# Input projection weights split by a casting DMA and an accumulating DMA

## The chip, the cores and the metric

The kernel runs on one core of one Trainium2 chip. The metric is the device time of one launch in microseconds (us). PE is TensorE's matmul, PEld its weight load, DVE is VectorE, ACT is ScalarE, POOL is GpSimd, SP is SyncE, which here only issues DMAs.

## What is computed

One decoder block over 1024 tokens of width 1024: a LayerNorm, one combined input projection to 5648 columns, a state-space branch and a convolution branch on its columns, one output projection, and two norms with a gated per-layer input. What the change touches is the projection:

```
h    = layer_norm(x, ln_emb_g, ln_emb_b)
proj = einsum('bld,de->ble', h, w_in[i])
xs, z, bm, cm, dt_raw, glu, cgate = split(proj, SPLITS)
xbc  = silu(causal_depthwise_conv(concatenate([xs, bm, cm])))      # width 4
u    = (glu[:D] + b) * sigmoid(glu[D:] + b)
u    = silu(layer_norm(causal_depthwise_conv(u, ...)))             # width 31
```

## The kernel before, in words

Everything is float32. A matmul operand is split into two parts: `h` is the operand rounded to the 12 bits that TensorE's fast float32 form (`F32R`) takes, `l` is the exact rest. `three` (L122) then makes one product out of three matmuls: rest by rounded, rounded by rest, rounded by rounded (L123, L124, L125). `split` (L117) makes the two parts: ACT casts (L119), another engine subtracts (L120).

*Input projection.* The weights are 44 tiles of 128 output columns; each is [128, 8, 128] numbers, 512 KB, contiguous per partition in DRAM. `weights(ct)` (L182) takes three slots from a ring of eight (pool `regB`, tag `B2`): `wraw`, `wh`, `wl`. SP loads `wraw`, ACT casts it to `wh`, POOL subtracts to get `wl`. `inproj` (L188) runs 48 matmuls per tile, for two halves of 512 tokens and eight blocks of the input, into a PSUM bank (three banks with that tag), and ACT empties the bank after each half (L262, L265, L296, L373, L383). The input `h` and its parts `hH`, `hL` stay in SBUF.

*What runs beside it.* `ple_all` (L213) projects the per-layer input first; its two `ppraw` tiles take two of the eight slots for a while. `embed` (L159) normalises x (DVE, some on ACT; POOL takes the reciprocal root, L132 and L134), PE transposes it, DVE splits it. Then eight `conf_tile(j)` (L254): two projections each, a gate, and the convolution of width 31, on DVE (L291), but for tiles 1 and 5 as 30 ACT products (L285) and 30 POOL additions (L286). Between them stand two further steps each from a list: `dt_path`, `decays`, twelve `xbc_tile` (short convolution on DVE, L377, then SiLU on ACT, L378, and a store from SP, L379) and `z_tile`. POOL adds up the channel sums `cs` (L628, L630); `conf_norm` (L386) starts with PE's mean of them (L390). Then come the chunked scan and the output projections.

*What sets the order.* Each engine works through its own queue in order; a waiting instruction holds up what stands behind it on its engine. The order in each queue and the semaphores come from a planner that simulates the program when it is built; it can place work of a later step ahead of an earlier one. SP's queue holds all DMA issues of the program.

Of the kernel before, what the change touches and what calls it, by code (L numbers as in the profile page):

```python
# [8 lines left out]
F32 = mybir.dt.float32  # L9
F32R = mybir.dt.float32r  # L10
AF = mybir.ActivationFunctionType
# [3 lines left out]
P = 128  # L15
# [10 lines left out]

# columns of the per-channel vectors
VEC = {}
# [18 lines left out]
def tile_block(ctx: ExitStack, tc: tile.TileContext, x, pT, wple, win, wdt, wout, wgate, vec, rows, heads, out):  # L47
# [17 lines left out]

# [1 line left out]
    BUFS = {"gt": 4, "xd": 2, "u": 2, "ha": 3, "y": 2, "xb": 2, "st": 1}  # L67
# [19 lines left out]

# [1 line left out]
    vc = const.tile([P, NVEC], F32, name="vc")  # L89
# [13 lines left out]
    nc.gpsimd.memset(mhalf, -0.5)  # L103
    # [s, l]: 1 where l >= s
    tri = const.tile([P, P], F32, name="tri")
    nc.gpsimd.affine_select(out=tri, in_=ones, pattern=[[1, P]], compare_op=ALU.is_ge, fill=0.0, base=0, channel_multiplier=-1)
    # adds rows h, 16 + h and 32 + h
    fold = const.tile([P, HEADS], F32, name="fold")
# [8 lines left out]
    def split(src, h, l, leng):  # L117
        """h: src rounded to the tensor engine's 12 bits; l: what is left, exactly."""
        nc.scalar.copy(out=h.bitcast(F32R), in_=src)  # L119
        leng.tensor_tensor(out=l.bitcast(F32R), in0=src, in1=h, op=ALU.subtract)  # L120
# [16 lines left out]
    def moments(src, tag):  # L137
        """mean and rstd of the rows of src [P, 1024]."""
        st = wk.tile([P, 2, 6], F32, name="st" + tag, tag="st" + tag)
        for i in range(2):  # L140
            nc.vector.bn_stats(out=st[:, i, :], in_=src[:, i * 512:(i + 1) * 512])
        mv = small("mv" + tag, 2)
        nc.vector.bn_aggr(out=mv, in_=st)
        return mv[:, 0:1], rstd_of(mv[:, 1:2], 1, tag, nc.gpsimd)
# [6 lines left out]

# [1 line left out]
    xts = [regB.tile([P, D], F32, name="xt", tag="B1") for t in range(NT)]  # L153
# [26 lines left out]

# [1 line left out]
    def weights(ct):  # L182
        raw, wh, wl = (regB.tile([P, NK, P], F32, name=n, tag="B2") for n in ("wraw", "wh", "wl"))
        nc.sync.dma_start(out=raw, in_=win[ct])
        split(raw, wh, wl, nc.gpsimd)
        return wh.bitcast(F32R), wl.bitcast(F32R)
# [13 lines left out]
    def residual():  # L200
        ag, abb, bob = (work(n, "ha") for n in ("ag", "abb", "bob"))
        for i, tl in enumerate((ag, abb, bob)):
            nc.sync.dma_start(out=tl, in_=rows[i:i + 1, :].broadcast_to([P, D]))
        nc.gpsimd.tensor_scalar(out=ag, in0=ag, scalar1=ALPHA, scalar2=0.0, op0=ALU.mult, op1=ALU.add)
        nc.gpsimd.tensor_scalar(out=abb, in0=abb, scalar1=ALPHA, scalar2=0.0, op0=ALU.mult, op1=ALU.add)
        nc.gpsimd.tensor_tensor(out=abb, in0=abb, in1=bob, op=ALU.add)
        # alpha * h + b_out, by tokens
        for t in range(NT):
            nc.gpsimd.tensor_tensor(out=xts[t], in0=xts[t], in1=ag, op=ALU.mult)
            nc.gpsimd.tensor_tensor(out=xts[t], in0=xts[t], in1=abb, op=ALU.add)  # L210
            nc.sync.dma_start(out=ha_d[t], in_=xts[t])

    def ple_all():  # L213
        """the projected per-layer input, by tokens."""
        parts = {}
        tags = iter(["u", "u", "xd", "xd", "gt", "gt", "ha", "ha"])
        for src, nm in ((wple, "wp"), (pT, "pp")):
            for k in range(2):
                raw = work(nm + "raw", "xb") if nm == "wp" else regB.tile([P, L], F32, name=nm + "raw", tag="B2")
                parts[nm, k] = (raw, work(nm + "H", next(tags)), work(nm + "L", next(tags)))  # L220
        for half in range(2):
            hs = slice(half * 512, half * 512 + 512)
            for k in range(2):
                for src, nm in ((wple, "wp"), (pT, "pp")):
                    nc.sync.dma_start(out=parts[nm, k][0][:, hs], in_=src[:, k, hs])
                    split(*(a[:, hs] for a in parts[nm, k]), nc.vector)
        embed_load(0)
        nc.sync.dma_start(out=vc, in_=vec)
        nc.vector.tensor_scalar(out=hb, in0=v("bglu", 0, 16), scalar1=0.5, scalar2=None, op0=ALU.mult)
        parts = {i: (a[1].bitcast(F32R), a[2].bitcast(F32R)) for i, a in parts.items()}  # L230
        for t in range(NT):
            tk = slice(t * P, (t + 1) * P)
            pl = work("pl", "xb" if t % 4 > 1 else "y", L)
            for n in range(2):
                nn = slice(n * 512, n * 512 + 512)
                ps = bank("psp")
                for k in range(2):
                    three(ps, parts["pp", k][0][:, tk], parts["pp", k][1][:, tk], parts["wp", k][0][:, nn], parts["wp", k][1][:, nn], k == 0, k == 1)
                if (t + n) % 2:
                    nc.vector.tensor_copy(out=pl[:, nn], in_=ps)  # L240
                else:
                    nc.scalar.copy(out=pl[:, nn], in_=ps)
            nc.sync.dma_start(out=ple_d[t], in_=pl)
# [10 lines left out]
    def conf_tile(j):  # L254
        """GLU and the causal convolution of 128 channels."""
        ga = work("ga", "gt")
# [44 lines left out]
    def dt_path():  # L301
# [7 lines left out]
        nc.sync.dma_start(out=hd, in_=heads.unsqueeze(0).broadcast_to([P, 2, HEADS]))  # L309
        # both parts of the weights side by side  # L310
        nc.scalar.copy(out=wh2[:, :, 0:HEADS].bitcast(F32R), in_=raw)
# [22 lines left out]

        # softplus(v) = max(v, 0) + 2 atanh(e / (2 + e)), e = exp(-|v|)
        nc.vector.tensor_tensor(out=b3(vv), in0=b3(pst[:, 0:P]), in1=bh(hd[:, 0, :]), op=ALU.add)
# [16 lines left out]
    def decays():  # L353
        """dec holds dt * a at first: its sums over the tokens of each chunk, and what follows from them."""
        ar, er = (wk.tile([P, P], F32, name=n, tag="dg") for n in ("ar", "er"))
# [60 lines left out]
    def out_weight(src, get, tag, last, scale=None, leng=nc.gpsimd):  # L416
        """last: a place for the raw one, where those that share the tag leave none."""
        raw = work("wor", last) if last else get("wor", tag)
        nc.sync.dma_start(out=raw, in_=src)
        h, l = get("woh", tag), get("wol", tag)  # L420
        if scale is None:
            split(raw, h, l, leng)
        else:
            nc.scalar.activation(out=h.bitcast(F32R), in_=raw, func=AF.Copy, scale=scale)
            nc.vector.scalar_tensor_tensor(out=l.bitcast(F32R), in0=raw, scalar=scale, in1=h, op0=ALU.mult, op1=ALU.subtract)
        return h.bitcast(F32R), l.bitcast(F32R)

# [1 line left out]
    state = work("state", "st")  # L429
# [8 lines left out]
    def prep(c):  # L438
        """what chunk c needs besides the state: decays times C.B, x * dt, B by tokens."""
        xb = slabs(work("xb", "xb", 12 * P), 12)  # L440
# [8 lines left out]
        for q in range(2):  # L449
            er = ea_d[c * HEADS:(c + 1) * HEADS, :].rearrange("(t q) l -> q t l", q=2)[q]  # L450
            nc.sync.dma_start(out=ea[q * HD:(q + 1) * HD], in_=er.unsqueeze(0).broadcast_to([HD, NK, P]))
        # exp(acs[l] - acs[s]); the part l < s is held at exp(0) here and dropped with C.B
        for h in range(HEADS):
# [30 lines left out]
    def chunk(c, sz, xb, gg, ea, xdt, xdd, btok):  # L484
        y = slabs(work("y", "y"))
        for g in range(2):
            # from the state, scaled by exp(acs[l])
            ys = y[:, g * 4:g * 4 + 4, :]
# [34 lines left out]
    def mean_square(c, y, ea):  # L523
        """rstd of the two groups of channels of the gated output."""
        sq = ea.rearrange("p (g t) l -> p g t l", g=2)
# [21 lines left out]
    def conf_out(c, mH, mL, ha):  # L547
        """conformer half of the output projection"""
        for n in range(2):
# [14 lines left out]
    def affine(o, src, mu, rs, g, b):  # L564
        """(src - mu) * rs * g + b"""
        nc.vector.scalar_tensor_tensor(out=o, in0=src, scalar=mu, in1=g, op0=ALU.subtract, op1=ALU.mult)
        nc.vector.scalar_tensor_tensor(out=o, in0=o, scalar=rs, in1=b, op0=ALU.mult, op1=ALU.add)

    def out_proj(c, yH, yL):
        """the SSM half of the output projection, and the norm"""  # L570
        r = work("r", "ha")
# [21 lines left out]
    def gate(c, r, hTH, hTL):  # L593
        """the per-layer input, gated, and the norm"""
        pl = work("pl3", "st")
# [75 lines left out]

# [1 line left out]
    ready, last = out_proj(0, *ys.pop(0)), None  # L673
# [58 lines left out]
```

## Time and profile before

| | us |
|---|---|
| median of 3 runs | 932.74 (928.87 to 934.99) |
| profiled execution, span | 927.1 |
| PE busy | 877.1 |
| DVE busy | 708.6 |
| POOL busy | 534.4 |
| ACT busy | 364.8 |

The span goes from the first to the last instruction of the profiled execution; its time outside the span is not in the profile. A busy PE is not a PE at its peak, since matmuls overlap: a matmul's duration in the rows (about 390 ns) is longer than the distance between two starts. An idle time in the rows is put down to what ended it, and a wait for several things to what came last.

### The profile page before, as it was taken

How to read it: one execution, taken by the hardware profiler on the slowest of the kernel's cores; microseconds unless marked ns; L12 is line 12 of the kernel's file. 1: busy time of each engine (PE TensorE's matmuls, PEld its weight loads, DVE VectorE, ACT ScalarE, POOL GpSimd, SP SyncE). 2: the span in 40 equal slices, each digit the busy share in tenths (PEclk: the TensorE clock that was granted, in tenths of full speed). 3: DMA queues.
4: the chain of work that ended last, by engine and by line, in shares of the span. 5: the costliest groups of instructions: out<-in, count | busy, mean ns of one | idle time of the engine just before them, and what ended most of it. 6: DMA issues, size and time to landing. Idle time of an engine off the chain costs nothing.

```text
span 927.1 us, 10959 instructions
## 1 busy us (share of the span) xinstructions
PE 877.1 (95%) x4141; PEld 711.0 (77%) x4141; DVE 708.6 (76%) x830; ACT 364.8 (39%) x513; POOL 534.4 (58%) x298
## 2 busy tenths in 40 slices
PE   6989998989999999999899999999999889999996
PEld 5857787868787888788688887777777668888885
DVE  7868997498999989989626523998885786666665
ACT  3532244665423435555446533644343421111001
POOL 2559836999924249999792254676757442222211
PEclk9999999989999999999999999999999999999999
DMA  9703241321213121322322388888887902222111
GB/s 337 264 24 107 77 157 46 96 69 46 78 37 113 52 86 53 123 97 80 114 100 83 103 304 271 300 273 230 283 264 261 353 25 92 91 90 91 69 46 68
DMA packets 67716, 126.42 MB, mean 136 GB/s; under 512 B 4176, under 2 KB 41552, under 8 KB 67664
## 3 DMA queue, kind: packets, MB, share of 16 engines
q1 hardware_dynamic: 67664, 125.73, 40.4%
q8 instruction: 32, 0.52, 0.2%
q14 instruction: 20, 0.16, 0.1%
HBM read 89.93 MB, written 35.78 MB: 136 GB/s over the span
## 4 chain that ended last, share of the span: by engine, by line
PE 47%; DVE 20%; POOL 13%; DMA 11%; issue 6%; ACT 3%; SPq 1%; POOLq 0%; DVEq 0%; ACTq 0%
POOL acc L286 8%; DVE pc L291 7%; PE ps L123 6%; PE ps L124 6%; PE ps L125 6%; DVE cacc L377 4%; PE psg L123 3%; PE psg L125 3%; PE psg L124 3%; DMA wor<-in_wout_dram 3%; PE pss L123 3%; PE pss L125 3%; PE pss L124 3%; DMA xb<-xbc_d 2%; POOL wl L120 2%
## 5 line engine op out<-in xcount | busy, mean ns | idle before, releaser
L123 PE MATMUL ps<-hH,wl 128*128 128x512 f32 x704 | 278.4, 397 | 12.7 <-ACT ga L262 6.2
L124 PE MATMUL ps<-hL,wh 128*128 128x512 f32 x704 | 278.0, 395 | 1.0 <-DVE hL L179 1.0
L125 PE MATMUL ps<-hH,wh 128*128 128x512 f32 x704 | 278.1, 395 | 0.0
L291 DVE SCALAR_TENSOR_TENSOR pc<-u,vc,pc 128x1024 f32<-128x1024 f32 x174 | 223.8, 1286 | 4.5
L123 PEld LDWEIGHTS ps<-hH,wl 128*128 128x128 f32 x704 | 133.9, 191 | 44.7 <-issue 7.7
L286 POOL TENSOR_TENSOR acc<-acc,prod 128x1024 f32<-128x1024 f32 x60 | 160.2, 2671 | 13.3 <-ACT acc L282 9.3
L124 PEld LDWEIGHTS ps<-hL,wh 128*128 128x128 f32 x704 | 134.2, 191 | 29.3 <-DVE hL L179 1.5
L125 PEld LDWEIGHTS ps<-hH,wh 128*128 128x128 f32 x704 | 134.2, 191 | 28.4 <-issue 0.2
L120 POOL TENSOR_TENSOR wl<-wraw,wh 128x1024 fp32r<-128x1024 f32 x44 | 110.6, 2513 | 53.2 <-ACT wh L119 23.0
L132 POOL TENSOR_SCALAR ve<-mv 128x1 f32<-128x1 f32 x24 | 21.7, 907 | 121.3 <-DVE mv L611 88.4
L285 ACT ACTIVATE prod<-u,vc 128x1024 f32<-128x1024 f32 x60 | 68.8, 1150 | 51.4 <-POOL acc L286 44.9
L377 DVE SCALAR_TENSOR_TENSOR cacc<-xin,vc,cacc 128x1024 f32<-128x1024 f32 x36 | 76.9, 2135 | 7.4 <-ACT cacc L247 4.7
L119 ACT CAST wh<-wraw 128x1024 fp32r<-128x1024 f32 x44 | 46.2, 1051 | 82.6 <-DMA wraw<-in_win_dram 47.8
L455 DVE TENSOR_SCALAR gt<-gt,acs 128x128 f32<-128x128 f32 x128 | 42.0, 397 | 25.4 <-POOL qs L398 17.3
L123 PE MATMUL psg<-woh,hTL 128*128 128x512 f32 (+1 forms) x136 | 52.9, 389 | 4.8 <-DVE hTL L120 4.8
L123 PE MATMUL pso<-woh,mL 128*128 128x512 f32 x128 | 51.6, 406 | 2.8 <-POOL mL L120 1.8
L123 PE MATMUL pss<-woh,yL 128*128 128x512 f32 x128 | 50.8, 397 | 3.4 <-DVE r L580 3.4
L120 POOL TENSOR_TENSOR wol<-wor,woh 128x1024 fp32r<-128x1024 f32 x12 | 32.7, 2743 | 36.1 <-ACT woh L119 36.1
L125 PE MATMUL pso<-woh,mH 128*128 128x512 f32 x128 | 53.2, 417 | 0.0
L125 PE MATMUL psg<-woh,hTH 128*128 128x512 f32 (+1 forms) x136 | 52.6, 387 | 0.0
L124 PE MATMUL psg<-wol,hTH 128*128 128x512 f32 (+1 forms) x136 | 52.1, 383 | 0.0
L124 PE MATMUL pso<-wol,mH 128*128 128x512 f32 x128 | 50.9, 397 | 0.0
(184 smaller groups left out, 1435.5 us busy)
## 6 DMA issues: line engine op xcount, KB each, us to landing
wraw<-in_win_dram SPq DMA_DIRECT2D x44, 512.0 KB, 4.1
gt<-acs_d SPq DMA_DIRECT2D x16, 512.0 KB, 4.6
wor<-in_wout_dram SPq DMA_DIRECT2D x16, 512.0 KB, 6.1
xbc_d<-cacc SPq DMA_DIRECT2D x12, 512.0 KB, 3.4
xb<-xbc_d SPq DMA_DIRECT2D x8, 768.0 KB, 6.3
xt<-in_x_dram SPq DMA_DIRECT2D x8, 512.0 KB, 9.2
ple_d<-pl SPq DMA_DIRECT2D x8, 512.0 KB, 5.0
ha_d<-xt SPq DMA_DIRECT2D x8, 512.0 KB, 5.2
```

The lines of the kernel that those rows point to most:

```text
L119: nc.scalar.copy(out=h.bitcast(F32R), in_=src)
L120: leng.tensor_tensor(out=l.bitcast(F32R), in0=src, in1=h, op=ALU.subtract)
L123: mm(ps, lhsT=ll, rhs=rh, start=first, stop=False)
L124: mm(ps, lhsT=lh, rhs=rl, start=False, stop=False)
L125: mm(ps, lhsT=lh, rhs=rh, start=False, stop=last)
L132: eng.tensor_scalar(out=ve, in0=var, scalar1=EPS, scalar2=None, op0=ALU.add)
L285: nc.scalar.activation(out=pr, in_=u[:, i:i + L], func=AF.Copy, scale=v("ccw", j * KC + i))
L286: nc.gpsimd.tensor_tensor(out=acc, in0=acc, in1=pr, op=ALU.add)
L291: nc.vector.scalar_tensor_tensor(out=pc if i + 1 < KC else acc, in0=u[:, i:i + L], scalar=v("ccw", j * KC + i), in1=pc, op0=ALU.mult, op1= ...
L377: nc.vector.scalar_tensor_tensor(out=acc, in0=xin[:, j:j + L], scalar=v("scw", i * 4 + j), in1=acc, op0=ALU.mult, op1=ALU.add)
L455: nc.vector.tensor_scalar(out=sl, in0=sl, scalar1=col(acs, c, h), scalar2=0.0, op0=ALU.subtract, op1=ALU.min)
```

## The change

The raw tile is no longer loaded into a slot of its own. A DMA issued from POOL reads the weights from DRAM and casts them on the way into `wh`; ACT writes the negative of `wh` into `wl`; a second DMA issued from POOL reads the same weights from DRAM again and adds them onto `wl`. A tile takes two slots of the ring instead of three, and 1024 KB of reads from DRAM instead of 512. The other lines of the diff remove comments.

```diff
     def weights(ct):
-        raw, wh, wl = (regB.tile([P, NK, P], F32, name=n, tag="B2") for n in ("wraw", "wh", "wl"))
-        nc.sync.dma_start(out=raw, in_=win[ct])
-        split(raw, wh, wl, nc.gpsimd)
+        wh, wl = (regB.tile([P, NK, P], F32, name=n, tag="B2") for n in ("wh", "wl"))
+
+        nc.gpsimd.dma_start(out=wh.bitcast(F32R), in_=win[ct])
+        nc.scalar.activation(out=wl.bitcast(F32R), in_=wh, func=AF.Copy, scale=-1.0)
+        nc.gpsimd.dma_start(out=wl.bitcast(F32R), in_=win[ct], accum_op=ALU.add)
         return wh.bitcast(F32R), wl.bitcast(F32R)
```

## Rows read from the trace of the kernel before

**Rows 1.** The page: span, and PE's busy us (share) x instructions.
```profile
span 927.1 us, 10959 instructions
PE 877.1 (95%) x4141; PEld 711.0 (77%) x4141; DVE 708.6 (76%) x830; ACT 364.8 (39%) x513; POOL 534.4 (58%) x298
```

**Rows 2.** Stretches: length, then PE, PEld, DVE, ACT, POOL busy, PEclk, DMA, GB/s.
```profile
60.00:136.00 76.00, 73.84 (x321) 57.21 (x320) 67.19 (x59) 23.11 (x29) 48.83 (x21) 0.96 0.31 111
136.00:250.00 114.00, 107.09 (x454) 87.14 (x453) 92.14 (x63) 61.16 (x67) 102.82 (x46) 0.96 0.20 62
250.00:340.00 90.00, 88.45 (x388) 72.26 (x387) 88.56 (x71) 31.65 (x38) 29.11 (x18) 1.00 0.26 81
340.00:456.00 116.00, 113.09 (x494) 92.11 (x493) 101.71 (x75) 62.08 (x81) 113.61 (x47) 0.99 0.29 89
456.00:568.00 112.00, 112.00 (x515) 92.77 (x515) 46.21 (x83) 53.50 (x59) 49.83 (x21) 1.00 0.44 149
```

**Rows 3.** Timeline of a quiet stretch: start, duration (us), engine, line, operation.
```profile
300.17 0.39 PE L124 MATMUL ps<-hL,wh 128*128 128x512 f32 x1
...
311.05 0.39 PE L124 MATMUL ps<-hL,wh 128*128 128x512 f32 x1
```

**Rows 4.** The tile wl: duration ns min/median/max, first to last start (us).
```profile
L123 PE MATMUL ps<-hH,wl x704: 387/389/763, 36.5 to 566.8; 128*128 128x512 f32 x176
```

**Rows 5.** PE's waits, 60 to 545 us: total us, times, longest.
```profile
PE ps L123 <- ACT ga L262: 6.2, 4, 3.5
PE ps L123 <- ACT xin L373: 3.7, 3, 2.6
```

**Rows 6.** ACT's waits.
```profile
ACT cacc L378 <- DVE cacc L377: 68.8, 11, 13.5
ACT wh L119 <- DMA wraw<-in_win_dram: 47.8, 14, 8.9
ACT prod L285 <- POOL acc L286: 44.9, 39, 2.2
ACT wh L119 <- POOL wl L120: 31.1, 15, 7.6
```

**Rows 7.** Timeline of POOL and of PE where the channel sums end.
```profile
449.74 4.85 POOL L630 TENSOR_TENSOR cs<-cs,acc 128x1024 f32<-128x1024 f32 x2
...
454.64 1.98 PE L390 MATMUL mu<-cs,invd 128*128 128x512 f32 x4 [0.58 <-POOL cs L630]
```

**Rows 8.** Groups by line, whole span: busy us, mean ns, idle us before them.
```profile
L120 POOL TENSOR_TENSOR wl<-wraw,wh 128x1024 fp32r<-128x1024 f32 x44 | 110.6, 2513 | 53.2 <-ACT wh L119 23.0 <-PE ps L123 22.1 <-issue 4.9
...
L119 ACT CAST wh<-wraw 128x1024 fp32r<-128x1024 f32 x44 | 46.2, 1051 | 82.6 <-DMA wraw<-in_win_dram 47.8 <-POOL wl L120 31.1 <-POOL xin L372 3.4
...
L132 POOL TENSOR_SCALAR ve<-mv 128x1 f32<-128x1 f32 x24 | 21.7, 907 | 121.3 <-DVE mv L611 88.4 <-DVE mv L143 31.3 <-DVE wh L312 1.6
```

**Rows 9.** Groups by line, 340 to 456 us.
```profile
L120 POOL TENSOR_TENSOR wl<-wraw,wh 128x1024 fp32r<-128x1024 f32 x11 | 27.4, 2488 | 0.0
```

**Rows 10.** The line L377: duration ns min/median/max, first to last start.
```profile
L377 DVE SCALAR_TENSOR_TENSOR cacc<-xin,vc,cacc x36: 1276/2222/3473, 95.8 to 376.3; 128x1024 f32<-128x1024 f32 x36
```

**Rows 11.** The tile wraw: SP's issues (ns), and landing after issue.
```profile
L184 SPq DMA_DIRECT2D wraw<-in_win_dram x44: 327/332/1482, 9.6 to 524.2; - x44
...
DMA to landing us min/median/max: 3.2/4.1/8.2
```

**Rows 12.** The waits of SP's queue.
```profile
SPq L184 <- PE ps L125: 139.5, 21, 13.2
```

**Rows 13.** POOL's waits, 0 to 545 us.
```profile
POOL wl L120 <- ACT wh L119: 23.0, 6, 9.4
POOL wl L120 <- PE ps L123: 22.1, 3, 9.2
```

**Rows 14.** The first 20 us; columns as in the stretches above.
```profile
0.00:20.00 20.00, 12.03 (x39) 9.13 (x40) 13.06 (x24) 8.86 (x13) 3.30 (x17) 1.00 0.90 326
```

**Rows 15.** The tile xt: DVE's normalising passes (ns).
```profile
L167 DVE TENSOR_SCALAR xt<-xt,mv,rs x6: 796/804/809, 15.4 to 31.7; 128x1024 f32<-128x1024 f32 x6
```

## The prediction

> **What bounds the kernel now.** I read the page first: PE is busy 95% of the span, far ahead of the others [rows 1]. The change touches only the weights of the input projection, so I cut the span at its ends and at the ends of POOL's two busy stretches [rows 2]. What comes after 568 us issues none of the changed instructions; it can only begin earlier or later.
>
> Is a busy PE in the projection at its limit? In a quiet stretch one matmul starts at 300.17 and another, 48 matmuls on, at 311.05 us [rows 3]: 0.227 us each, 10.88 us for one tile of 128 output columns (8 blocks x 3 products x 2 halves). 44 tiles are 478.7 us; the projection's first and last matmuls start at 36.5 and 566.8 us [rows 4]. So most of these 530 us is matmul at its own pace, and other matmuls (transposes, the preparation of the chunks, the means) fill part of what is left. What is to be won between 60 and 568 us is small. PE's busy times in the five stages sum to 494.5 of 508 us [rows 2]: 13.5 us idle. The granted clock is 0.96, 0.96, 1.00, 0.99 and 1.00, which loses 3.0 + 4.6 + 0 + 1.2 + 0 = 8.8 us. 22.3 us is the whole prize.
>
> Who makes the holes? PE's waits name ACT above all, 6.2 + 3.7 = 9.9 us: PE has no free bank because ACT empties one late [rows 5]. ACT is late because it stands in order behind its own waits: for DVE's short convolution (68.8 us), for the raw weights (47.8), for POOL's additions (44.9), for POOL's subtraction to free a slot (31.1) [rows 6]. So the weights reach PE mostly by way of ACT's queue.
>
> The other queue to read is POOL's. From 136 to 250 and from 340 to 456 us it is busy 102.8 of 114 and 113.6 of 116 us [rows 2]: in each it adds up one convolution tile, with subtractions for the weights in between. At the end of the second stretch POOL ends the last channel sum at 454.59 us, and PE starts the mean at 454.64 after an idle 0.58 us [rows 7]. There POOL's queue already sets PE's time, though it costs almost nothing yet.
>
> **The change, part by part.**
> *Removed from POOL:* 44 subtractions of 2.51 us, 110.6 us [rows 8]; 11 of them, 27.4 us, in the stretch from 340 to 456 us [rows 9].
>
> *Added to POOL:* 88 DMA issues. The trace holds no DMA issued from POOL. From below, SP's issue of the same load takes 0.33 us [rows 11]; from above, a whole POOL pass over the tile, 2.51. I take 0.9, by the row it is nearest to: an issue handles one address for each of 128 rows, and POOL's instruction on one number in each of 128 rows takes 0.91 [rows 8]. In the second stretch 22 x 0.9 = 19.8 us stand against 27.4 + 2.4 idle = 29.8 us; 10.0 us remain for waiting. The ends: 22 x 0.33 = 7.3 (22.5 us to spare), 22 x 2.51 = 55.2 (25.4 too many).
>
> *The waits that come with them.* SP waited for PE to free a slot, 139.5 us in all [rows 12]; now POOL waits for that, and once more until ACT has negated. Behind such a wait stand POOL's additions; ACT's products, and at last PE's mean, wait for those. Before, POOL waited in front of its subtractions 23.0 us for ACT and 22.1 for PE [rows 13]: 45.1 / 88 = 0.51 us for each issue that replaces them, if the pattern stays. In the second stretch 22 x 0.51 = 11.3, less the 10.0 to spare: **+1.3 us** at the mean. Ends: no wait, POOL ends early and wins PE's 0.6 us there; or each accumulating issue stands out a landing and ACT's pass, 4.1 + 1.05 = 5.15 us a tile [rows 8, 11].
>
> *The path of one tile.* Eight slots held two and two thirds triples and now hold four pairs, so a new pair has three tiles of PE, 32.6 us, to get ready. It needs 0.9 + a landing + ACT's 1.05 + 0.9 + a second landing. A plain load lands after 3.2 to 8.2, median 4.1 us [rows 11]. For the cast I take 4.1. The accumulation reads two tiles and writes one: from 3.2 (as a plain load) to 16.4 (twice the slowest); I take 8.2, since it reads twice as much. Sum 15.2, at the ends 9.3 and 27.5; all are below 32.6, so PE sees no late weights while POOL keeps pace. The Trainium skill (DMA: Bandwidth & Descriptors, Anatomy of one DMA) gives a DMA issued from GpSimd about 2.0 us plus its bytes over 436 GB/s, here about 3.2 us (an estimate from that page). With two such landings the path is 9.3 instead of 15.2 us, and the time forecast the same; no run so far shows a DMA issued there.
>
> *DMA bytes:* 44 x 0.52 MB more, 23 MB, some 45 GB/s over 508 us. The stages move 62 to 149 GB/s [rows 2] and the first 20 us show 326 [rows 14]: hidden, unless the casting or adding engine is several times slower (a rival).
>
> *ACT:* 44 casts of 1.05 us go [rows 8], 44 negations of a tile of the same size come: nothing. Its waits for raw weights and their slots, 78.9 us, are 41% of the 192.6 us above. If holes and slow clock fall in that share: 0.41 x (9.9 + 8.8) = 7.7 us. But ACT now waits for the cast to land, so I keep half: **-3.8 us**; ends 0 and -22.3.
>
> *SP and DVE* are relieved: SP of 44 issues, DVE where its short convolution stands beside POOL's passes (1.28 us at the shortest, 2.22 in the median, 3.47 at the longest [rows 10]) and the subtractions are gone. Both are off PE's path; what they give shows as shorter ACT waits, counted above.
>
> *The start.* The DMA engines are busy 0.90 of the first 20 us at 326 GB/s [rows 14]. The casts no longer queue behind x on SP. Three pairs fit beside the two slots of the per-layer input: 3.1 MB instead of the first two raw loads, 1.0 MB. If those 2.1 MB all go ahead of x, x is 6.4 us late and so is all behind it; if none does, 0. I take **+2 us**, a third, since x needs only some of these microseconds to come first.
>
> **The sum.** +1.3 - 3.8 + 2 = -0.5: a span of 926.6 us. The page does not give the profiled execution's time around its span; the median of the runs lies 5.6 us above the span (their ends 1.8 and 7.9). 926.6 + 5.6 = 932.2, predicted 932 us.
>
> **Rivals.**
> *POOL's queue becomes the pace (slower, 0.30).* Place: 340 to 456 us. If each accumulating issue stands out half a landing and pass, 2.6 us a tile, 11 tiles cost 28.6 less 10.0, 18.6 us, and the mean is late by that: 932.2 - 1.3 + 18.6 = 950. A whole one: 56.7 - 10.0 = 46.7, 978. It decides from 0.45 us of wait per issue; past 1% it needs 0.96. For it: POOL has only 2.4 us idle there, and ACT, which must negate, also feeds POOL's additions in the same queue. Against: in front of its subtractions in that stretch POOL waited 0.0 us [rows 9].
>
> *The holes close (faster, 0.20).* ACT is relieved, issues cost 0.33 us, nothing is lost elsewhere: half to all of 22.3 us, 921.5 to 910.4. For it: 9.9 us of the holes are ACT's. Against: ACT's largest wait, for DVE, has another cause.
>
> *The start slips (0.05).* The whole 6.4 us, and issues held up by DVE: each of its six normalising passes of 0.80 us [rows 15] holds one, 4.8 us. 932.2 - 2 + 11.2 = 941, still inside 1%. The Trainium skill (SBUF — State Buffer, Who interferes with whom) states such a rule: VectorE in a two-port mode locks GpSimd out, and descriptor generation starves. No row here can show it, as no DMA is generated there.
>
> *The transfers are slow (slower, 0.02).* A tile's two must fit in 10.88 us; 0.52 MB at 326 GB/s is 1.6 us each, so they must be over three times slower. At five times, 16 us a tile: 44 x 5.1 = +225 us, 1157.
>
> **How the numbers follow.** About 1% is what a measurement of this kernel can tell from no change. Forecast 0.43, its own range 924 to 941; with the slipped start, within 1%: 0.48. Faster 0.20, slower 0.30 + 0.02 = 0.32. From 918 to 965 leaves out the better part of the closed holes (0.06), the longer waits of POOL (0.09) and the slow transfers (0.02).
>
> **What would show it.** POOL's DMA issues at about 0.9 us; landings near 4 us for the cast and 8 for the accumulation; PE's idle time from 60 to 568 us near 11 us, ended by ACT; POOL's last channel sum ending between 450 and 460 us; DVE's short convolution below 2.2 us. PE waiting for the mean by over 5 us, or weight loads waiting for a DMA, would make me wrong.

## The result

| | median of 12 runs, us | lowest to highest |
|---|---|---|
| before | 931.78 | 928.87 to 936.24 |
| changed | 937.65 | 934.63 to 941.03 |

The ratio is 1.0054, with a 95% interval of 1.0032 to 1.0076: slower by 0.54%, some 5 us, where 932 us was forecast. A later series of the same two kernels gave 1.0070 (1.0047 to 1.0093).

A word on the profiles: in the changed kernel's 12 runs the time less the span is 1.65 to 1.77 us. The profiled execution of before (927.1 + 1.7) was the lowest of its 12 runs, that of the changed kernel (938.2 + 1.7 = 939.9) a high one, so the 11 us between the spans are twice the real difference. Of these 11, 4.8 us lie ahead of the projection's last matmul (572.06 instead of 567.29 us) and 6.3 behind it, where no line was changed: there the granted clock of the changed kernel is 0.93 from 700 to 750 and from 750 to 800 us, in a second profile of it too, and 1.00 and 0.97 before. No experiment looks at that part, and what of it belongs to the change stays open. A profile is read below for where time is lost up to the projection's end, the ratios for how much.

**The stretches.** First the stages of [rows 2], in the same columns, of the changed kernel:

```profile
60.00:136.00 76.00, 64.29 (x281) 49.64 (x281) 68.73 (x62) 15.44 (x20) 38.72 (x25) 0.91 0.45 132
136.00:250.00 114.00, 104.81 (x451) 85.38 (x450) 85.34 (x58) 66.25 (x73) 95.08 (x57) 0.96 0.46 101
250.00:340.00 90.00, 90.00 (x399) 74.53 (x398) 88.70 (x72) 31.24 (x38) 15.84 (x25) 1.00 0.58 129
340.00:456.00 116.00, 116.00 (x517) 95.48 (x516) 106.83 (x82) 59.39 (x68) 99.30 (x57) 1.00 0.59 140
113.00:118.00 5.00, 4.99 (x12) 3.94 (x13) 5.00 (x7) 1.09 (x2) 0.65 (x2) 0.50 0.78 165
102.00:120.00 18.00, 7.33 (x22) 5.60 (x21) 18.00 (x19) 8.35 (x10) 6.94 (x8) 0.62 0.51 100
```

From 250 to 456 us PE has no idle time left: 4.5 us less than before. From 60 to 136 us it is idle for 11.7 us instead of 2.2, from 136 to 250 for 9.2 instead of 6.9. The last row is why in the first of the two: in 18 us PE works 7.33, at a mean clock of 0.62. The projection's matmuls start at 40.2 us instead of 36.5 [rows 4], the third tile's at 79.18 instead of 77.41, and the last one comes 4.8 us later than before. So a gain in the dense stretches was eaten by two holes.

**The two holes.** PE's waits up to 560 us:

```profile
PE ps L123 <- DMA wl<-in_win_dram: 10.7, 1, 10.7
PE ps L123 <- ACT xin L375: 9.2, 3, 7.2
```

One wait of 10.7 us for a weight tile, of which [rows 5] has none, and one of 7.2 for ACT. The timeline of the changed kernel around them, in the order POOL, DVE, ACT, PE (L185 issues the cast, L186 negates, L187 issues the accumulation; L212 adds the residual's `abb` in eight additions that follow each other on POOL, called the run below):

```profile
79.79 0.62 POOL L185 DMA_DIRECT2D wh<-in_win_dram  x1
...
86.36 0.58 POOL L185 DMA_DIRECT2D wh<-in_win_dram  x1 [0.36 <-issue]
86.97 18.75 POOL L212 TENSOR_TENSOR xt<-xt,abb 128x1024 f32<-128x1024 f32 x8
107.52 0.91 POOL L187 DMA_DIRECT2D wl<-in_win_dram  x1 [1.80 <-ACT wl L186]
...
89.62 16.25 DVE L339 SCALAR_TENSOR_TENSOR dt<-dt 128x128 f32<-128x128 f32 x1
...
143.90 1.22 DVE L281 SCALAR_TENSOR_TENSOR u<-tb,ga 128x1024 f32<-128x1024 f32 x1
...
105.96 0.31 ACT L340 ACTIVATE dt<-dt 128x128 f32<-128x128 f32 x1 [20.54 <-DVE dt L339]
106.18 1.04 ACT L186 ACTIVATE wl<-wh 128x1024 fp32r<-128x1024 f32 x1
...
145.21 1.24 ACT L284 ACTIVATE acc<-u,vc 128x1024 f32<-128x1024 f32 x1 [17.96 <-DVE u L281]
...
149.38 0.56 ACT L375 COPY xin<-ps 128x512 f32<-128x512 f32 x1
...
113.01 0.77 PE L123 MATMUL ps<-hH,wl 128*128 128x512 f32 x1 [10.67 <-DMA wl<-in_win_dram]
113.57 0.63 PE L124 MATMUL ps<-hL,wh 128*128 128x512 f32 x1
114.00 0.63 PE L125 MATMUL ps<-hH,wh 128*128 128x512 f32 x1
```

The first hole: POOL issues the cast of the fifth tile at 79.79, then works through the run, and only then, at 107.52, issues the accumulation that completes the tile. PE has been idle since 102.3. When it starts again, matmuls begin 0.43 us apart, not 0.227 [rows 3]: from 113 to 118 us the granted clock is 0.50, the lower of its two levels (1.2 GHz).

The second hole begins at the same run. A DVE instruction on 128 numbers a partition, about 0.3 us elsewhere, stands for 16.25 us, until the additions are over. DVE's long convolution behind it ends late, so does `u` at 143.90, ACT waits 18 us for that, and behind it in ACT's queue stands the copy that empties PE's bank.

The same place in the kernel before: the fifth tile's subtraction stood ahead of the run (and, between the two, a fill of 0.09 us), and DVE got turns between POOL's passes (first POOL, then one of DVE's longest there, a pass of 1.28 us that waited some 2.1):

```profile
83.77 2.39 POOL L120 TENSOR_TENSOR wl<-wraw,wh 128x1024 fp32r<-128x1024 f32 x1
86.17 21.03 POOL L210 TENSOR_TENSOR xt<-xt,abb 128x1024 f32<-128x1024 f32 x8
...
95.78 3.41 DVE L377 SCALAR_TENSOR_TENSOR cacc<-xin,vc,cacc 128x1024 f32<-128x1024 f32 x1
```

**The prices.** The cast and the accumulation on POOL (issue ns min/median/max; group: busy us, mean ns, idle before), and the landings of both and of x (KB, us):

```profile
L185 POOL DMA_DIRECT2D wh<-in_win_dram x44: 546/594/966, 2.4 to 528.8; - x44
...
L187 POOL DMA_DIRECT2D wl<-in_win_dram x44 | 38.6, 878 | 114.4 <-ACT wl L186 92.6
...
wh<-in_win_dram POOLq DMA_DIRECT2D x44, 512.0 KB, 4.3
wl<-in_win_dram POOLq DMA_DIRECT2D x44, 512.0 KB, 5.4
...
xt<-in_x_dram SPq DMA_DIRECT2D x8, 512.0 KB, 11.5
```

### The profile page after: what moved, and what is told of

It is laid out like the page before. It is cut to its first block, busy times and chain, and to the rows that moved or that the text cites. A ratio compares the mean times of both kernels' runs of the same rounds, so it can differ in the third digit from the quotient of the medians.

```text
span 938.2 us, 10969 instructions
## 1 busy us (share of the span) xinstructions
PE 877.2 (94%) x4141; PEld 713.1 (76%) x4141; DVE 692.9 (74%) x830; ACT 362.7 (39%) x513; POOL 479.7 (51%) x342
## 4 chain that ended last, share of the span: by engine, by line
PE 48%; DVE 20%; DMA 10%; POOL 10%; issue 8%; ACT 3%; SPq 0%; POOLq 0%; DVEq 0%; ACTq 0%
DVE pc L293 8%; PE ps L124 6%; PE ps L125 6%; PE ps L123 6%; POOL acc L288 5%; PE psg L123 3%; DVE cacc L379 3%; PE psg L125 3%; PE psg L124 3%; PE pss L123 3%; PE pss L125 3%; PE pss L124 3%; DMA wh<-in_win_dram 2%; PE pso L123 2%; DVE dt L339 2%
## 5 line engine op out<-in xcount | busy, mean ns | idle before, releaser
L123 PE MATMUL ps<-hH,wl 128*128 128x512 f32 x704 | 277.3, 395 | 21.1 <-DMA wl<-in_win_dram 10.7
L123 PEld LDWEIGHTS ps<-hH,wl 128*128 128x128 f32 x704 | 133.1, 190 | 51.0 <-issue 11.3
L288 POOL TENSOR_TENSOR acc<-acc,prod 128x1024 f32<-128x1024 f32 x60 | 156.3, 2605 | 9.3 <-issue 3.5
L187 POOL DMA_DIRECT2D wl<-in_win_dram x44 | 38.6, 878 | 114.4 <-ACT wl L186 92.6
L132 POOL TENSOR_SCALAR ve<-mv 128x1 f32<-128x1 f32 x24 | 21.6, 902 | 120.7 <-DVE mv L613 89.2
L379 DVE SCALAR_TENSOR_TENSOR cacc<-xin,vc,cacc 128x1024 f32<-128x1024 f32 x36 | 65.8, 1827 | 14.5 <-ACT cacc L249 14.4
L186 ACT ACTIVATE wl<-wh 128x1024 fp32r<-128x1024 f32 x44 | 46.5, 1057 | 73.3 <-DMA wh<-in_win_dram 73.2
L457 DVE TENSOR_SCALAR gt<-gt,acs 128x128 f32<-128x128 f32 x128 | 38.5, 373 | 26.9 <-DMA gt<-acs_d 26.9
L120 POOL TENSOR_TENSOR wol<-wor,woh 128x1024 fp32r<-128x1024 f32 x12 | 32.6, 2736 | 37.4 <-ACT woh L119 34.9
## 6 DMA issues: line engine op xcount, KB each, us to landing
xt<-in_x_dram SPq DMA_DIRECT2D x8, 512.0 KB, 11.5
```

The lines of the kernel that those rows point to most:

```text
L123: mm(ps, lhsT=ll, rhs=rh, start=first, stop=False)
L132: eng.tensor_scalar(out=ve, in0=var, scalar1=EPS, scalar2=None, op0=ALU.add)
L186: nc.scalar.activation(out=wl.bitcast(F32R), in_=wh, func=AF.Copy, scale=-1.0)
L187: nc.gpsimd.dma_start(out=wl.bitcast(F32R), in_=win[ct], accum_op=ALU.add)
L288: nc.gpsimd.tensor_tensor(out=acc, in0=acc, in1=pr, op=ALU.add)
L379: nc.vector.scalar_tensor_tensor(out=acc, in0=xin[:, j:j + L], scalar=v("scw", i * 4 + j), in1=acc, op0=ALU.mult, op1=ALU.add)
```

## Which hole has which cause

Three theories for the loss stood at the start: Q, the accumulation is late because of its place in POOL's queue; V, it is late because ACT's negation stands behind the held DVE instruction; S, the later start. Ratios below are to the kernel before, run beside each, with the 95% interval; `...` in a diff marks lines left out.

**Start alone.** The first two tiles as before, the other 42 changed (the 22 below is a slip).

```diff
...
-            wa, wb = weights(T_GA), weights(T_GB)
+            wa, wb = weights(T_GA, True), weights(T_GB, True)
```

> The first two tiles of the projection (ga and b of channel tile 0) are loaded and split as in the kernel before; the other 22 keep the casting and the accumulating DMA. If the later start is a cost of its own, because the two casts go ahead of x and x lands later, the projection's first matmul goes back from 40.2 us to about 36.5 us, and the time is 3 to 4 us under the changed kernel's 937.65, at about 934, still with the hole of PE at 102 to 113 us. If the start is swallowed later, by a wait that ends at a fixed time whatever the start was (the hole, which ends when the fifth tile's accumulate has landed behind the residual's eight additions on POOL), the first matmul is early and the time stays at 937 to 938, with the hole longer by what the start gained.

1.0054 (1.0028 to 1.0081), as the changed kernel itself. The first matmul is at 37.2 us, but that lead is gone before the hole. PE waits 3.2 us for DVE's part of `h`, from 61 to 66 us the granted clock is 0.50, and the third tile starts at 81.01 us, later than in the changed kernel (79.18). The hole is as long and ends no sooner:

```profile
60.81 0.79 PE L124 MATMUL ps<-hL,wh 128*128 128x512 f32 x1 [3.20 <-DVE hL L179]
...
114.70 0.77 PE L123 MATMUL ps<-hH,wl 128*128 128x512 f32 x1 [10.53 <-DMA wl<-in_win_dram]
```

An earlier first matmul alone brings nothing back, so S in that form does not explain the loss. What a start that stays early would be worth, this run does not show.

**DVE's instruction taken out of the way of ACT.**

```diff
-        nc.vector.scalar_tensor_tensor(out=e, in0=vv, scalar=-1.0, in1=vv, op0=ALU.mult, op1=ALU.min)
-        nc.scalar.activation(out=e, in_=e, func=AF.Exp)
+        nc.scalar.activation(out=e, in_=vv, func=AF.Abs)
+        nc.scalar.activation(out=e, in_=e, func=AF.Exp, scale=-1.0)
```

> The changed kernel with one VectorE instruction less in the dt phase: e = -|v|, which stood 16.25 us (89.62 to 105.87) beside POOL's run of eight additions, is made by ScalarE (Abs, then Exp with scale -1). POOL's order of work is the same. Theory Q, POOL's queue: the fifth tile's accumulating DMA stands behind the eight additions (86.97 to 105.7) in POOL's own queue, so it can be issued no earlier than about 105.7 us; the edit saves at most the 1.80 us that its issue then waited for ScalarE's negation, PE's hole of 10.67 us stays at 8.9 or more, and the time is 936 to 938. Theory V, ScalarE's queue behind the VectorE instruction: with the VectorE instruction gone the negation is done by about 82 us and the hole goes with it; the time is 10 to 12 us lower, about 926.

1.0045 (1.0019 to 1.0072). The negation was done by 91.6 us; the accumulation was still issued at 107.09, behind the run, and the first hole is 2 us shorter, about what Q allowed (1.8). V falls with it as the cause of the first hole. DVE was held all the same, at its next instruction (a form with one input), and the second hole stayed:

```profile
91.06 16.18 DVE L341 TENSOR_SCALAR dt<-dt 128x128 f32<-128x128 f32 x1
...
112.36 0.77 PE L123 MATMUL ps<-hH,wl 128*128 128x512 f32 x1 [8.62 <-DMA wl<-in_win_dram]
...
151.34 0.79 PE L123 MATMUL ps<-hH,wl 128*128 128x512 f32 x1 [9.37 <-ACT xin L375]
```

**The run behind the fifth tile's accumulation,** alone and with the early start.

```diff
-            nc.gpsimd.tensor_tensor(out=xts[t], in0=xts[t], in1=abb, op=ALU.add)
+            with tc.issue_after(adds[T_GB + 1]):
+                nc.gpsimd.tensor_tensor(out=xts[t], in0=xts[t], in1=abb, op=ALU.add)
...
+            for ct in (T_B, T_GA + 1, T_GB + 1):
+                ahead_w[ct] = weights(ct)
             residual()
```

> The changed kernel with an issue order alone: the residual's additions of abb (eight of POOL, 18.75 us) stand behind the accumulating DMA of the fifth tile (gb of channel tile 1) in POOL's queue instead of ahead of it; the weights of the third, fourth and fifth tile are asked for that much earlier in the program. Theory Q, POOL's queue: the accumulate is issued at about 85 to 88 us, its landing 5.4 us later is ahead of PE, the hole of 10.67 us at 102 to 113 us is gone and with it the half-speed matmuls up to 118 us: 10 to 13 us under the changed kernel, 925 to 928, and so some 4 to 7 us under the kernel before. Theory V, ScalarE's queue: the negation still waits for the VectorE instruction of dt wherever that one is held, and the hole moves with it; the time is within 3 us of 937.65. A third case: the additions pushed back stand ahead of the sixth or seventh tile's accumulate instead, and a hole of 5 to 10 us opens some 10 to 20 us later; the time is 932 to 938.

> Both edits together: the first two tiles the old way, and the residual's additions behind the fifth tile's accumulating DMA. If the start (3.7 us) and the hole (10.7 us and about 2.5 us of half-speed matmuls) are the two costs and the rest of the change a gain of about 12 us between 136 and 568 us, the time is 13 to 16 us under the changed kernel: 921 to 925, about 8 to 10 us under the kernel before. If the start is swallowed by a later wait, it is no lower than the kernel with the order alone; if the dense stretches gained only because the hole ahead of them let POOL and ScalarE get ahead, the gain of 136 to 568 us shrinks as the hole goes, and the time is 930 to 936.

The order alone: 1.0018 (0.9992 to 1.0044); with the early start: 0.9960 (0.9940 to 0.9981), 927.83 us, which is none of the three times expected. The hole at 102 us is gone, which is Q; but the run now stands ahead of the next tiles' accumulations and holds DVE, so the third case came, two holes further on (the order alone):

```profile
120.28 0.79 PE L123 MATMUL ps<-hH,wl 128*128 128x512 f32 x1 [6.31 <-ACT ga L269]
...
140.83 0.77 PE L123 MATMUL ps<-hH,wl 128*128 128x512 f32 x1 [6.55 <-DMA wl<-in_win_dram]
...
95.09 17.16 DVE L348 TENSOR_TENSOR dt<-dt 128x128 f32<-128x128 f32 x1
```

So it is the run as such that must not stand between a cast and its accumulation.

## What is left when the run is out of the way

**The first eight tiles as before,** the other 36 changed: POOL's order through the run is that of the kernel before.

```diff
...
+        count[0] += 1
+        if count[0] <= 8:
+            raw, wh, wl = (regB.tile([P, NK, P], F32, name=n, tag="B2") for n in ("wraw", "wh", "wl"))
+            nc.sync.dma_start(out=raw, in_=win[ct])
+            split(raw, wh, wl, nc.gpsimd)
+            return wh.bitcast(F32R), wl.bitcast(F32R)
```

> The first eight tiles of the projection are loaded and split as in the kernel before, the other 36 by the two DMAs: POOL's order through the residual's eight additions is that of the kernel before. If the loss sits in the start and in that stretch (first matmul 3.7 us later; PE's holes of 10.67 us at 102 and 7.15 us at 143, both behind the run of eight additions), and the rest of the change is a gain, then the first matmul is at about 36.5 us, the holes at 113 and 151 us are those of before (2.0 and 2.6), PE is full from 250 to 456 us as in the changed kernel, and the time is 921 to 926, 5 to 10 us under the kernel before. If the dense stretches were full only because the holes ahead of them had let the other engines catch up, the holes of before come back there and the time is 929 to 932.

0.9872 (0.9838 to 0.9906), 919.22 us, under the 921 to 926 expected. The holes of before at 111 and 148 us are there (1.9 and 2.8 us), DVE is not held, and from 250 to 456 us PE is full. The rest of the change is a gain of 11 us.

**The run in pairs,** each pair behind one accumulation, the weights of six tiles asked for ahead of it, with the early start.

```diff
...
+            with tc.issue_after(adds[(T_GB + 1, T_B + 1, T_B + 2, T_GA + 2)[t // 2]]):
...
+            for ct in (T_B, T_GA + 1, T_GB + 1, T_B + 1, T_B + 2, T_GA + 2):
+                ahead_w[ct] = weights(ct)
```

> The changed kernel with the first two tiles the old way, and the residual's eight additions not in one run on POOL but in pairs, each pair behind the accumulating DMA of the fifth, sixth, seventh and eighth tile. Theory R, the run: eight additions in a row keep the accumulating DMAs behind them waiting for 19 us and hold one VectorE instruction for 16 to 17 us (dt's, 89.62 to 105.87 in the changed kernel), and behind that ScalarE. Then no VectorE instruction beside a pair takes longer than about 5 us, no hole of PE between 60 and 160 us is over 4 us, the projection's last matmul starts at 555 to 560 us instead of 571.8, and the time is 919 to 925. If VectorE's hold and ScalarE's lag come from something else (the DMA issues on POOL), holes of 6 to 7 us as with the order alone (120 and 141 us) stay, and the time is 926 to 930.

0.9901 (0.9863 to 0.9938), 921.99 us. PE has no hole between 61 and 129 us, so the accumulations came in time. The time is the one that theory R gave, but its sign is not there: DVE was held beside the pairs, over the DMA issues between two of them as well, 9.25 and later 9.88 us, and a hole ended by ACT stayed at 130 to 136 us:

```profile
94.71 9.25 DVE L353 TENSOR_TENSOR dt<-dt 128x128 f32<-128x128 f32 x1
...
136.23 0.80 PE L123 MATMUL ps<-hH,wl 128*128 128x512 f32 x1 [6.30 <-ACT xin L385]
```

**Each half of the change alone.**

```diff
 accumulation alone
         nc.sync.dma_start(out=raw, in_=win[ct])
-        split(raw, wh, wl, nc.gpsimd)
+        nc.scalar.copy(out=wh.bitcast(F32R), in_=raw)
+        nc.scalar.activation(out=wl.bitcast(F32R), in_=wh, func=AF.Copy, scale=-1.0)
+        nc.gpsimd.dma_start(out=wl.bitcast(F32R), in_=win[ct], accum_op=ALU.add)
 cast alone
         nc.sync.dma_start(out=raw, in_=win[ct])
-        split(raw, wh, wl, nc.gpsimd)
+        nc.gpsimd.dma_start(out=wh.bitcast(F32R), in_=win[ct])
+        nc.gpsimd.tensor_tensor(out=wl.bitcast(F32R), in0=raw, in1=wh, op=ALU.subtract)
```

> The second half of the change alone: SyncE loads the raw weights and ScalarE rounds them as before; wl is made as -wh on ScalarE and an accumulating DMA from POOL (no casting DMA; ScalarE has 44 more activations of 1.04 us, POOL 44 subtractions of 2.51 us less). In its order the accumulating DMAs of the fourth and fifth tile stand ahead of the residual's eight additions. If the accumulating DMA as such were slow for PE, the loss of the changed kernel is here too: 936 or more. If only its place behind the additions costs, the hole at 102 to 113 us is gone and the start is that of before, and the time is 923 to 929, less what ScalarE's 46 us more bring back (up to 4 us).

> The first half alone: wh by a casting DMA from POOL, the raw weights still loaded by SyncE, the subtraction still on POOL (ScalarE 44 casts of 1.05 us less, POOL 44 DMA issues of about 0.59 us more). POOL's queue as the pace from 340 to 456 us, where it had 27.4 of 116 us for weights and no idle time of its own: 10 more issues there add about 6 us, so the mean of the channel sums comes later than in before and the time is 935 to 940. If POOL had room, or ScalarE's casts were what held PE at its holes (13 of the idle microseconds end with ScalarE), the time is 926 to 931.

The accumulation alone: 0.9878 (0.9835 to 0.9920), 920.67 us. Its stage from 60 us, and POOL ahead of the run:

```profile
60.00:136.00 76.00, 76.00 (x346) 60.17 (x346) 68.66 (x68) 29.79 (x35) 38.74 (x21) 1.00 0.55 153
...
81.15 0.89 POOL L187 DMA_DIRECT2D wl<-in_win_dram  x1
82.21 0.86 POOL L187 DMA_DIRECT2D wl<-in_win_dram  x1 [0.17 <-issue]
83.84 0.10 POOL L374 MEMSET xin<- 128x3 f32 x1 [0.76 <-PE pstd L328]
83.90 20.03 POOL L212 TENSOR_TENSOR xt<-xt,abb 128x1024 f32<-128x1024 f32 x8
```

The wraw tiles come from SP long ahead, so the accumulations of the fourth and fifth tile fit in front of the run, and PE is full. The time is at the low end of what was expected, with ACT's 46 us more in it.

The cast alone: 1.0267 (1.0216 to 1.0318), 954.07 us, beyond both expectations. POOL keeps its 44 subtractions and gets 44 issues; DVE is held for 17.77 us beside the run; PE waits 11.3 us in one piece for ACT at 154 us. What of the 24 us is POOL's queue and what the hold, this run does not tell apart.

## What holds DVE

In the kernels so far DVE was held for 16 to 18 us wherever the whole run stood right behind a DMA issue of POOL (or behind an issue and a fill of 0.1 us, in the cast alone); not in the kernel before, nor with the first eight tiles as before, nor with the accumulation alone, where POOL had stood idle for 0.76 us after the last issue. Two kernels test that: the issue moved behind the run in the changed kernel, and an idle DMA put into the kernel before.

```diff
 changed kernel, cast of the sixth tile behind the run
-        nc.gpsimd.dma_start(out=wh.bitcast(F32R), in_=win[ct])
+        with tc.issue_after(run[0]) if ct == T_B + 1 else nullcontext():
+            nc.gpsimd.dma_start(out=wh.bitcast(F32R), in_=win[ct])
...
 kernel before, an idle DMA between the first and second addition
...
+            if t == 0:
+                with tc.issue_after(first):
+                    probe = nc.gpsimd.dma_start(out=idle, in_=win[0][:, 0, 0:1]).ins
```

> The changed kernel with one DMA issue of POOL moved: the sixth tile's cast, which stood directly ahead of the residual's eight additions, comes directly behind them. So far a VectorE instruction was held for 16 to 18 us in the kernels whose run of eight stands right behind a DMA issue (the changed one, the start alone, Abs, both orders) and in the cast alone, where the issue and a 0.1 us fill of xin stand ahead of it; it was not in the kernel before, with the first eight tiles the old way, and with the accumulate alone, where two accumulates, a wait of POOL for PE and a fill stand ahead. Theory I, the issue ahead of the run brings the hold: no VectorE instruction between 86 and 107 us takes over 4 us, the run of eight takes 20 to 21 us instead of 18.75, the hole at 143 to 150 us shrinks from 7.15 to about 3 us, the hole of 10.7 us stays (the fifth tile's accumulate is still behind the run), and the time is 3 to 5 us under the changed kernel's, at a ratio of 1.000 to 1.003. Theory M, it is the moment at which VectorE asks: the hold stays, 16 us, and the time is that of the changed kernel (ratio 1.0054) or a little over, since the sixth tile comes later.

> The kernel before with one DMA of POOL more, which nothing uses (128 words, into a tile of its own), issued between the first and the second of the residual's eight additions; the other seven follow it directly. Theory I, the issue ahead of the run brings the hold: a VectorE instruction beside the seven additions takes 10 to 15 us, the seven take 16.4 us (2.34 each) without a turn for VectorE, PE's hole at 151 us grows from 2.6 to about 7 us, and the time is 2 to 6 us over the kernel before. Theory M: no VectorE instruction there takes over 4 us, and the time is within 1 us of the kernel before.

> The changed kernel itself once more, beside the two others and the same runs of the kernel before. What its first profile showed should be there again if it belongs to the kernel: the first matmul at 40 us, the hole of 10 to 11 us for wl, a VectorE instruction of dt held for about 16 us, the hole of 7 us at 143 to 150 us, and a ratio of 1.003 to 1.008. A hold that came by chance in one execution would be gone or of another length.

*Issue moved away:* 1.0025 (1.0001 to 1.0048). The run takes 19.96 us, DVE gets its turns (its longest is again the 1.28 us pass that waited 2.1), the second hole is gone; the first, 12.2 us, is there. DVE works in the same order as in the changed kernel up to `u` and beyond. POOL, DVE, PE:

```profile
86.70 19.96 POOL L215 TENSOR_TENSOR xt<-xt,abb 128x1024 f32<-128x1024 f32 x8
...
98.67 3.41 DVE L382 SCALAR_TENSOR_TENSOR cacc<-xin,vc,cacc 128x1024 f32<-128x1024 f32 x1
...
137.29 1.22 DVE L284 SCALAR_TENSOR_TENSOR u<-tb,ga 128x1024 f32<-128x1024 f32 x1
...
115.28 0.77 PE L123 MATMUL ps<-hH,wl 128*128 128x512 f32 x1 [12.21 <-DMA wl<-in_win_dram]
```

`u` comes at 137.29 instead of 143.90: the second hole was the hold's.

*Idle DMA added:* 1.0075 (1.0050 to 1.0101), 936.72 us. One DMA of 128 words that nobody waits for costs 7 us, more than the 2 to 6 expected. POOL, DVE, PE:

```profile
86.14 0.75 POOL L216 DMA_DIRECT2D idle<-in_win_dram  x1
86.92 16.50 POOL L213 TENSOR_TENSOR xt<-xt,abb 128x1024 f32<-128x1024 f32 x7
...
87.47 18.39 DVE L345 TENSOR_SCALAR dt<-dt 128x128 f32<-128x128 f32 x1
...
118.28 0.77 PE L123 MATMUL ps<-hH,wl 128*128 128x512 f32 x1 [9.15 <-ACT ga L268]
```

The seven additions follow each other without a turn for DVE, 2.36 us each, and the subtraction behind them too; then POOL has nothing to do and DVE goes on. So the hold is longer than the 10 to 15 us expected. The hole opened at another place than I had said, 118 us and not 151: it is the hole that the kernel before has at 113.40 us, 1.95 us long and ended by the same step of ACT (`ga`); ahead of that step ACT waits here for DVE's short convolution for 20.7 us instead of 13.5, and the hole is 9.15 us long. Theory I holds for the run: an issue right ahead of it brings the hold. Moving the issue also moved the moment at which DVE asks, from 2.65 to 3.66 us behind the run's begin, so that kernel alone would leave theory M open. The rest of the record speaks against M: in the kernel before, DVE's instructions asked 0.1 to 2.25 us into an addition and all got a turn, and the held ones asked 0.3 (changed kernel), 0.6 (idle DMA) and 2.2 us (pairs) into one.

*Where an issue did not bring it.* In POOL's convolution stretches of the changed kernel many issues stand right ahead of additions. None of DVE's 36 short-convolution passes, most of them beside such additions, took over 3.42 us, so none waited more than 2.2 (POOL, DVE, then all 36 passes, min/median/max in ns):

```profile
358.19 0.84 POOL L185 DMA_DIRECT2D wh<-in_win_dram  x1
358.80 6.03 POOL L288 TENSOR_TENSOR acc<-acc,prod 128x1024 f32<-128x1024 f32 x2
...
359.84 2.72 DVE L379 SCALAR_TENSOR_TENSOR cacc<-xin,vc,cacc 128x1024 f32<-128x1024 f32 x1
...
L379 DVE SCALAR_TENSOR_TENSOR cacc<-xin,vc,cacc x36: 1277/1284/3415, 110.5 to 380.1; 128x1024 f32<-128x1024 f32 x36
```

These additions each take a product that ACT has just made, the residual's take nothing that is still to come, and the passes are longer than the held instructions. Which of this makes the difference, no run here shows; an issue right ahead is not enough by itself.

*The changed kernel once more:* 1.0070, first matmul at 41.4 us, holes of 10.72 and 6.77 us, the same instruction held for 16.22. The two holes and the hold belong to the kernel.

## What the start may cost, and a better version

The first two tiles the new way or the old way, in the kernel with the run in pairs:

> The kernel with the residual's additions in pairs, but with the first two tiles by the two DMAs as in the changed kernel (so its first matmul is at about 40 us again). If the later start is a cost of its own once no hole behind it swallows it, the time is 2.5 to 4 us over the same kernel with the first two tiles the old way, which stands beside it, and the projection's last matmul is later by as much. If it is swallowed here too (by the wait for xin at 130 to 136 us, which ends with VectorE's dt work), the two are within 1.5 us, and the hole there is shorter by what the start lost.

> The additions in pairs with the first two tiles the old way, once more, on the same chip and against the same runs as the kernel with the late start: a ratio of 0.987 to 0.993 as before, first matmul at 37 us, a hole of about 6 us at 130 to 136 us.

New way 0.9975 (0.9949 to 1.0000), 928.21 us; old way 0.9941 (0.9918 to 0.9964), 923.69, outside the 0.987 to 0.993 expected, for a kernel that gave 0.9901 in the earlier series. The medians are 4.5 us apart, the intervals overlap a little. With the order alone the early start was worth 3.9 us (931.75 and 927.83), under the first hole nothing. The profiles do not show such a cost: the lead of the old way (36.85 and 40.39 us) is gone by the third tile (80.66 and 79.95), through the same 3.2 us wait for DVE and the half clock behind it as in the start alone, and in each pair the projection's last matmuls lie within 0.5 us of each other. The executions of one kernel lie 6 to 11 us apart in these four, so one profile of each can't settle it. The medians put some 4 us on the start in two of three pairs; whether the start is what costs them stays open.

**A mix.** The first eight tiles with the accumulation alone, the other 36 as changed:

```diff
...
+        if count[0] <= 8:
+            raw, wh, wl = (regB.tile([P, NK, P], F32, name=n, tag="B2") for n in ("wraw", "wh", "wl"))
+            nc.sync.dma_start(out=raw, in_=win[ct])
+            nc.scalar.copy(out=wh.bitcast(F32R), in_=raw)
+            nc.scalar.activation(out=wl.bitcast(F32R), in_=wh, func=AF.Copy, scale=-1.0)
+            nc.gpsimd.dma_start(out=wl.bitcast(F32R), in_=win[ct], accum_op=ALU.add)
+            return wh.bitcast(F32R), wl.bitcast(F32R)
```

> A mix of what did best so far: the first eight tiles loaded by SyncE, rounded and negated on ScalarE and completed by the accumulating DMA (no casting DMA before x and none ahead of the residual's run), the other 36 as in the changed kernel, so that ScalarE is rid of 36 casts of 1.05 us. It should have the full stretch from 60 to 136 us of the accumulate alone (PE 76.0 of 76) and the full stretches from 250 us of the changed kernel. If both add up: the projection's last matmul at 548 to 551 us and the time 916 to 920, 1 to 4 us under the accumulate alone. If ScalarE's casts cost nothing any more once the holes are gone, it is level with it at 919 to 922.

0.9838 (0.9808 to 0.9869), 913.43 us: some 15 us under the kernel before and better than I had expected. PE is busy for 74.4 of 76 us from 60 us and for 116.0 of 116 us from 340 us.

## The prediction, point by point

**The step that failed** is the path of one tile: "all are below 32.6, so PE sees no late weights while POOL keeps pace". The path itself was over-costed (0.59 + 4.3 + 1.06 + 0.88 + 5.4 = 12.2 us, forecast 15.2). But it took the second issue to come when its data are ready. It is an instruction in POOL's queue, and between it and the first stood 18.75 us of additions. The subtraction that it replaces had its data early and stood ahead of them. I asked of POOL's queue only whether its sum fits, in the one stretch where POOL is full, and spread the waits evenly, 0.51 us an issue. The hole fell into a stretch where POOL is half idle, 38.7 of 76 us. My own sign of being wrong, weight loads that wait for a DMA, is what the profile shows. The second hole has no term in the sum either: what POOL's issues do to DVE beside them I put at nothing.

**That the time still lies in my own range** of 924 to 941 us is luck. With the first eight tiles as before the change gains 1.3%; between that kernel (0.9872) and the changed one (1.0054) lie some 17 us that these eight tiles lose, and neither stands in the sum at that size.

**POOL at the mean, +1.3 us:** did not come. Issues and waits together were near the sum, 16.6 + 13.6 = 30.2 us against the 29.8 that were free. The issues took 0.70 and 0.87 us on average there, and their waits 13.6 us for 21, 0.65 each, 1.24 a tile; the pace rival's 950 us needed 2.6 a tile. The last sum ended at 451.81 us (454.59 before, [rows 7]) and PE did not wait:

```profile
L187 POOL DMA_DIRECT2D wl<-in_win_dram x11 | 9.6, 872 | 13.5 <-ACT wl L186 13.5
L185 POOL DMA_DIRECT2D wh<-in_win_dram x10 | 7.0, 696 | 0.1
...
449.15 2.66 POOL L632 TENSOR_TENSOR cs<-cs,acc 128x1024 f32<-128x1024 f32 x1
```

**The holes that close, -3.8 us:** came near where no run stands in the way, 4.5 us from 250 to 456. The rival's 921.5 to 910.4 us holds in the kernels without the run's holes (919, 921, 913). What kept it from showing in the changed kernel is the failed step.

**The start, +2 us:** 3.7 us at the first matmul, in my range of 0 to 6.4, and 1.8 by the third tile; x landed after 11.5 us instead of 9.2. The rival beside it had DVE hold up POOL's issues; none took over 0.98 us in the changed kernel, so this did not come. What came is the other direction. The Trainium skill (SBUF — State Buffer, Who interferes with whom) says that of GpSimd and a VectorE in a two-port mode whichever issues first has the shared ports for the whole instruction. The kernel before agrees with one instruction (DVE waited 2.2 us at most, an addition takes 2.4). In the changed kernel the order is borne out, the length is not: 16.25 us were seven of POOL's additions, not one, and there the measurement decides. Whether the held instructions run in such a mode, no run here shows.

**DVE's short convolution** below 2.2 us: 1.28 in the median (2.22 before), right. **PE's idle time** near 11 us from 60 to 568: 21.6, wrong by the two holes. **The landings:** 4.3 where I took 4.1, 5.4 instead of 8.2; the 3.2 us worked out beside them are under both. **The time around the span:** I read 5.6 us where it is 1.7; the rest was that the profiled execution lay under the median. The forecast, 0.5 us under the median of before, is not changed by it.

## What to carry to other kernels

When one instruction becomes two with a transfer between them, follow the second one to its place in its queue and look for the longest run of other work that can fall in between; whether the queue has room on average says nothing of it. Ask it in every stretch, also where the engine is half idle: both holes here came from one place of 44. And where DVE works beside a run of POOL's passes that wait for nothing, look whether a DMA issue of POOL stands right ahead of it. Here it helped to move the issue behind the run, to load from SP, or that POOL stood idle for 0.76 us in between; a fill of 0.1 us in between did not help.

## What the hardware showed that I had not expected

With no DMA issue right ahead, a DVE instruction beside the residual's eight POOL additions of 128x1024 waited 2.2 us at most and then had its turn (five kernels; the run took 19.96 to 21.03 us). With one right ahead, a DVE instruction was held until POOL's passes there were over: 16.2 to 18.4 us over a run, 9.25 to 9.88 us over two pairs and the one or two issues between them; the run of eight took 18.75 to 19.16 us. Forms with one and with two inputs were held alike. Beside POOL's convolution additions, also right behind an issue, the short convolution waited 2.2 us at most. Why an issue changes who gets the turn, and why not there, no run here shows.
